# A two-layer hybrid backbone on one core: a different opening, loads moved to GpSimd's queue, and two spacings changed

## The chip, the cores and the metric

The kernel runs on one NeuronCore of a Trainium2 chip. The metric is the device time of one execution in microseconds. TensorE (PE) multiplies matrices, VectorE (DVE), ScalarE (ACT) and GpSimd (POOL) do elementwise work, and SyncE (SP), ScalarE and GpSimd issue DMAs, each into a queue of its own. An engine works through its instructions in the order of the program; an instruction that waits holds up all that stands behind it on that engine.

## The reference, cut to what matters

Two layers work on 256 context tokens and 256 latent tokens of width 1024. Each layer is a mixer of four branches and an MLP, both behind a modulated RMS norm. Context tokens go through the first layer whole; in the second only their scan states are needed.

```python
for l in range(DEPTH):                                  # DEPTH = 2
    mod   = c_act  @ w_mod[l] + b_mod[l]                # shift, scale, gate of both halves, latent tokens
    mod_c = cc_act @ w_mod[l] + b_mod[l]                # the same for context tokens
    hc = _modulate(xc, g_norm1[l], csh1, csc1)          # rms_norm(x, g) * (1 + scale) + shift
    zc = hc @ w_in[l]                                   # 1024 -> 5*256 branch inputs + 4*1024 gates
    ctx_states = _s5_states(zc[..., :256], *s5p, None)  # complex diagonal scan, both directions
    xc = xc + cga1 * _token_mixer(zc, ctx_states, p)    # (first layer only)
    xc = xc + cga2 * _sq_relu_mlp(_modulate(xc, g_norm2[l], csh2, csc2), mlp_w1[l], mlp_w2[l])
    h = _modulate(x, g_norm1[l], sh1, sc1)
    z = h @ w_in[l]
    lat_states = _s5_states(z[..., :256], *s5p, _s5_final(ctx_states))
    x = x + ga1 * _token_mixer(z, lat_states, p)        # S5, Fourier, pooling, convolution; gated, summed
    x = x + ga2 * _sq_relu_mlp(_modulate(x, g_norm2[l], sh2, sc2), mlp_w1[l], mlp_w2[l])
return _rms_norm(x, g_final)
```

The latent tokens get a 2-D position code added before the first layer.

## The kernel before

Activations lie transposed: 8 tiles of 128 channels by 512 tokens (context first, then latent), in `X`. Every large product takes three float32r products (high x high, high x low, low x high), so each weight tile (128 x 1024, 512 KB) is split after its load: ScalarE writes the high part, VectorE subtracts to get the low part. `Stream` does this for all weights in one fixed order with three raw buffers: `load` issues on SyncE's queue, `high` on ScalarE, and `low` on VectorE, which also frees the raw buffer for the next load. A low part is issued when its due time has come, or at the latest when `take` hands the weight to the products.

All instructions are put in order by the program itself. It keeps a clock for each engine ("t" TensorE, "d" VectorE, "a" ScalarE, "p" GpSimd), made of estimated costs. Between the products of a tile `pump` takes steps of background tasks, generators that say with `yield "w", x` that they want x us of TensorE's clock to pass, and that run when the clocks of their engines are less than a lead ahead of "t". So a step's place in every engine's queue follows from these estimates, and a wrong estimate shows up as an engine that stands still.

**The opening** (`run`, and the first part of `layer` for l = 0). x is loaded in four DMAs of two tiles, behind them weights and the 16 modulation pieces of 512 KB (`mod_load`, up to ten buffers). Position codes are added on VectorE, ScalarE squares, VectorE adds pairs, and each pair's sum goes to TensorE at once, which adds up all four pairs in one bank against a column of ones (`sums`). The norm's inverse root is a chain of small VectorE operations (`norm_steps`), and its broadcast goes over TensorE. `mod_part` multiplies one modulation piece; after each fourth, `mod_finish` turns the result into scale and shift of two of the eight tiles, which `h_tiles` needs to make the normed tiles. The first four column tiles of the input projection (two for S5, two for pooling) run k by k, as the tiles come: `group(k, *js)` does three products for each j. The order of groups, pieces, closings and tiles is written out by hand. `warm(n)` issues n products whose result isn't used.

**The first layer's mixer** goes through `order(0)`: gates (g), branch outputs (y) and projections (q), while background tasks make the branches. `S5.prep` (31 steps) makes the scan's discretised matrices, `tables_c` and `tables_b` (in rank order beside the others) its tables: four units u, for each of which a 64 KB piece of the C matrices is loaded (two buffers, SyncE's queue) and reloaded for u + 2 after unit u. The tables go out to DRAM. `S5L.run` starts when both are done. `states` loads the branch's input and four tables of 512 KB, into two buffers, on GpSimd's queue; the load for unit i + 2 is issued after the products of unit i. `mods_pe` computes the gate modulation of the first layer from eight pieces of 512 KB, one buffer, with a wait of 7.0 between a load and its products. `mods` does the rest of the modulation on VectorE until the MLP.

**The second layer's mixer** runs on the 256 latent tokens (context only for S5), so that a weight tile lasts half as long on TensorE, and its scan runs on VectorE beside the branches.

## Time and profile before

| | |
|---|---|
| time, median of 3 runs | 1208.14 us (1204.47 to 1208.62) |
| profiled execution: time, span, mean granted TensorE clock | 1212.6 us, 1210.8 us, 0.988 |
| TensorE busy | 1167.6 us, 96% |
| VectorE, ScalarE, GpSimd busy | 79%, 45%, 132.4 us |
| DMA | 211.50 MB, 175 GB/s on the mean |

A page of the profile gives the busy time of each engine (PEld is TensorE's load of the stationary operand, beside PE), the span in 40 slices and the costliest groups. The other views are asked for a stretch of time: a timeline of merged instructions, the list of waits, and tables of stretches with busy times and the granted clock. Nearly all instructions carry line 64, that of a helper that records them, so a group is told by the tiles that it reads and writes: "parts" are weight tiles and normed tiles, "mixer", "windows" and "scan" work areas, "whole" the area of x, raw weights and small things, "bank" PSUM. "in_..." and "scr_..." are tensors in DRAM.

### The profile page before, as it was taken

Reading aid. Unit: us, or ns where it says so; the run is one execution under the profiler, and the core shown is the slowest. Engines: PE = TensorE matmul, PEld = TensorE weight load, DVE = VectorE, ACT = ScalarE, POOL = GpSimd, SP = SyncE. Lnnn points to the kernel's source line nnn. Section 1 sums busy time; section 2 is a strip of 40 time slices with the busy share of each in tenths; the row PEclk is TensorE's granted clock in tenths of the full one; section 3 lists DMA queues with packets and bytes.
Section 4 is the critical chain, followed back from the end, with each engine's and each line's share of the span. In section 5 each row is a group of like instructions: output and inputs, shape, how many; then the busy total and the mean of one; then the engine's idle time right before and its main releaser. Section 6 shows DMA issues by size and latency. Waiting matters only on the chain. (4 is left out here: it accounts for less than half of the span.)

```text
span 1210.8 us, 20441 instructions
## 1 busy us (share of the span) xinstructions
PE 1167.6 (96%) x7900; PEld 1013.4 (84%) x7900; DVE 951.9 (79%) x1818; ACT 541.0 (45%) x1037; POOL 132.4 (11%) x134
## 2 busy tenths in 40 slices
PE   6899999999999999999999999999999999999997
PEld 5577676877877898888887778898989999999997
DVE  5587698997989768999988973557998788867764
ACT  4355543235333355332433442336644556645543
POOL 0010000000000100043324531030000002000000
PEclk9899999999999999999999999999999999999999
DMA  9363464337554603346777853435544546555551
GB/s 369 122 220 118 149 221 140 101 91 264 189 182 153 222 19 125 129 166 222 234 258 276 270 192 115 152 120 158 210 150 148 171 160 212 174 190 178 188 185 43
DMA packets 66370, 211.50 MB, mean 175 GB/s; under 512 B 7840, under 2 KB 13472, under 8 KB 66272
## 3 DMA queue, kind: packets, MB, share of 16 engines
q1 hardware_dynamic: 55456, 183.84, 44.7%
q10 hardware_dynamic: 7552, 14.56, 3.3%
q0 software_dynamic: 3264, 11.80, 2.9%
q8 instruction: 62, 1.02, 0.4%
q14 instruction: 36, 0.29, 0.1%
HBM read 199.19 MB, written 10.98 MB: 174 GB/s over the span
## 5 line engine op out<-in xcount | busy, mean ns | idle before, releaser
L64 PE MATMUL bank<-parts 128*128 128x512 f32 (+2 forms) x4008 | 728.0, 339 | 14.6 <-DVE parts L64 9.9
L64 PEld LDWEIGHTS bank<-parts 128*128 128x128 f32 x4008 | 613.1, 191 | 102.6 <-DVE parts L64 15.6
L64 ACT ACTIVATE parts<-whole 128x1024 fp32r<-128x1024 f32 (+1 forms) x288 | 273.6, 959 | 139.1 <-PE bank L64 63.5
L64 DVE TENSOR_TENSOR parts<-whole,parts 128x1024 fp32r<-128x1024 f32 (+1 forms) x240 | 292.2, 1225 | 16.0 <-ACT parts L64 15.3
L64 PE MATMUL bank<-hidden,parts 128*128 128x256 f32 (+1 forms) x1440 | 251.4, 335 | 0.0
L64 PEld LDWEIGHTS bank<-hidden,parts 128*128 128x128 f32 x1440 | 217.5, 188 | 29.7 <-issue 0.3
L64 DVE SCALAR_TENSOR_TENSOR whole<-whole 128x1024 f32<-128x1024 f32 (+3 forms) x174 | 158.5, 911 | 15.9 <-DMA whole<-in_w_modt_dram 12.8
L64 DVE SCALAR_TENSOR_TENSOR whole<-bank,whole 128x256 f32<-128x256 f32 (+1 forms) x121 | 54.8, 476 | 71.6 <-PE bank L64 71.6
L64 ACT ACTIVATE whole<-whole 128x256 f32<-128x256 f32 (+4 forms) x119 | 47.4, 423 | 96.7 <-DVE whole L64 96.3
L64 ACT ACTIVATE mixer<-bank 128x512 f32<-128x512 f32 (+1 forms) x84 | 40.6, 495 | 100.1 <-PE bank L64 92.9
L64 ACT ACTIVATE whole<-bank 128x512 f32<-128x512 f32 (+2 forms) x71 | 35.9, 527 | 106.2 <-PE bank L64 75.6
L64 DVE TENSOR_TENSOR whole<-whole 128x512 f32<-128x512 f32 (+7 forms) x154 | 62.7, 420 | 20.6 <-ACT whole L64 19.0
L64 POOL TENSOR_TENSOR whole<-whole 128x256 f32<-128x256 f32 (+2 forms) x42 | 30.1, 730 | 316.3 <-ACT whole L64 315.6
L64 DVE TENSOR_TENSOR hidden<-whole,hidden 128x512 fp32r<-128x512 f32 (+2 forms) x77 | 55.3, 722 | 9.4 <-ACT hidden L64 2.4
L64 ACT ACTIVATE hidden<-whole 128x512 fp32r<-128x512 f32 (+2 forms) x77 | 47.1, 615 | 6.5 <-PE bank L64 2.3
L64 DVE TENSOR_TENSOR scan<-scan 128x512 f32<-128x512 f32 (+3 forms) x51 | 28.4, 568 | 18.1 <-ACT scan L64 15.4
L64 DVE SCALAR_TENSOR_TENSOR scan<-scan,whole 128x512 f32<-128x512 f32 (+1 forms) x64 | 42.5, 733 | 0.0
L64 PE MATMUL bank<-merged,parts 128*128 128x256 f32 (+1 forms) x240 | 38.4, 317 | 1.3 <-DVE merged L64 1.3
L64 ACT ACTIVATE tables<-bank 128x512 f32<-128x512 f32 (+2 forms) x20 | 8.4, 420 | 67.5 <-PE bank L64 65.1
L64 POOL TENSOR_TENSOR whole<-tables 128x512 f32<-128x512 f32 x20 | 36.3, 1822 | 18.4 <-ACT tables L64 14.2
L64 PEld LDWEIGHTS bank<-merged,parts 128*128 128x128 f32 x240 | 33.8, 188 | 5.3 <-DVE merged L64 2.2
L64 DVE TENSOR_TENSOR mixer<-bank,mixer 128x512 f32<-128x512 f32 (+1 forms) x56 | 31.9, 575 | 7.5 <-PE bank L64 6.7
(109 smaller groups left out, 831.3 us busy)
## 6 DMA issues: line engine op xcount, KB each, us to landing
whole<-in_w_dram SPq DMA_DIRECT2D x128, 512.0 KB, 4.3
whole<-in_w_in_dram SPq DMA_DIRECT2D x84, 512.0 KB, 4.1
whole<-in_w_modt_dram SPq DMA_DIRECT2D x71, 512.0 KB, 4.3
whole<-in_w_br_dram SPq DMA_DIRECT2D x16, 512.0 KB, 3.9
whole<-in_w_out_dram SPq DMA_DIRECT2D x16, 512.0 KB, 4.1
mixer<-in_w_mod_dram SPq DMA_DIRECT2D x8, 512.0 KB, 8.2
whole<-in_w_modg_dram SPq DMA_DIRECT2D x8, 512.0 KB, 5.9
scan<-scr_b POOLq DMA_DIRECT2D x8, 512.0 KB, 6.3
```

Source lines behind the costliest of these rows:

```text
L64: return f(out, *a, **k)
```

## The change

- **Opening.** The position code of tiles 1, 3 and 5 is added on GpSimd, the sigmoid of the conditioning comes first, and the position tensor is loaded in two parts. The squares of all eight tiles are summed on VectorE into two accumulators, which TensorE then reduces in one go, behind two modulation pieces. The hand-written order of pieces, closings, tiles, groups and forced steps of S5's preparation is another; there are more warm products; the weights' loads come ahead of modulation pieces 4 to 7.
- **C matrices.** The first layer gets two more buffers, loads all four pieces at the start, and on GpSimd's queue.
- **Modulation pieces.** `mods_pe` loads on GpSimd's queue and waits 8.0 for a piece.
- **States.** In the first layer units 1 and 2 are followed by a wait of 5.0, not 1.0.
- **Low parts.** In the second layer's mixer a low part is due 0.5 after ScalarE's clock, where it was due 2.75 after TensorE's.
- A constant's load moves from the end of `mods` to the end of the first layer.

```diff
@@ -338,15 +338,17 @@
             CAs.append(K.MAT[:, 3072:3584])
+        else:
+            CCs += [A(128), A(128)]
         for BL in BLs:
...
         def load(u):
-            (nc.gpsimd if l else nc.sync).dma_start(CCs[u % 2], K.I["s5c"][l][u])
-
-        load(0)
-        load(1)
-        yield "w", 5.0 if l else 2.6
+            nc.gpsimd.dma_start(CCs[u % len(CCs)], K.I["s5c"][l][u])
+
+        for u in range(len(CCs)):
+            load(u)
+        yield "w", 5.0
@@ -372,11 +374,11 @@
             nc.scalar.dma_start(K.KD[l][64 * u:64 * u + 64], KK[0:64])
-            if u + 2 < 4:
-                load(u + 2)
+            if u + len(CCs) < 4:
+                load(u + len(CCs))
         def bufs(u, k):
-            CC = CCs[u % 2].rearrange("p (r k q c) -> p r k q c", r=2, k=2, c=16)
+            CC = CCs[u % len(CCs)].rearrange("p (r k q c) -> p r k q c", r=2, k=2, c=16)
             BL = BLs[u % nb].rearrange("p (k r q x) -> p k r q x", k=2, r=2, x=32)
@@ -499,7 +501,7 @@
                     nc.scalar.activation(o[:, :, ::-1] if k else o, pv[:, r, :, g], AF.Copy)
-            yield "w", 1.0
+            yield "w", 1.0 if l or i == 0 else 5.0
         if l == 0:
@@ -692,7 +694,7 @@
         self.ndma = self.nhigh = self.nlow = self.ntake = 0
-        self.used, self.due, self.lag = {}, [], 2.75
+        self.used, self.due, self.lag, self.early = {}, [], 2.75, False
@@ -717,7 +719,7 @@
                 self.nhigh += 1
-                self.due.append(self.K.nc.clock["t"] + self.lag)
+                self.due.append(self.K.nc.clock["a"] + 0.5 if self.early else self.K.nc.clock["t"] + self.lag)
                 return True
@@ -1105,7 +1107,6 @@
             yield "w", 3.02
-        nc.scalar.dma_start(self.MAT[:, 0:1792], self.I["const"][:, 264:2056])
         self.stream.free.append(self.MODRAW[0])
@@ -1117,8 +1118,8 @@
             for kp in range(4):
-                nc.sync.dma_start(raw, self.I["w_modg"][g][kp])
-                yield "w", 7.0
+                nc.gpsimd.dma_start(raw, self.I["w_modg"][g][kp])
+                yield "w", 8.0
                 for k in range(2):
@@ -1148,11 +1149,11 @@
...
-    def norm_steps(self, accs, n, width, d=None, pss=None):
+    def norm_steps(self, accs, n, width, d=None):
-        pss = pss or [self.aux() for _ in accs]
+        pss = [self.aux() for _ in accs]
@@ -1342,6 +1343,7 @@
         self.lead["d"] = 3.0 if l == 0 else 2.0
+        self.stream.early = l == 1
         s5 = S5L(self, l, self.pre[l])
@@ -1365,72 +1367,74 @@
-            prep = tab[0]
+            parts(2)
             weight(0)
-            norm = self.norm_steps((), 512, 1024, pss=[self.sums])
+            self.warm(1)
+            norm = self.norm_steps(((self.sq[1],), (self.sq[0],)), 512, 1024)
+            next(norm)
+            self.warm(2)
+            parts(1)
+            parts(1)
             y = [y for y in norm][-1]
-            parts(4)
+            self.warm(1)
+            self.mod_finish(0)
+            self.warm(2)
             d, r = self.tmp(), self.aux()
...
                 nc.tensor.matmul(r[:, sl], self.ones, d[:, sl], start=True, stop=True)
+            self.warm(4)
             h = self.h_tiles(l, 0, r, 0, 512)
             next(h)
-            self.mod_finish(0)
-            self.warm(2)
             next(h)
             group(0, 0)
+            self.stream.advance(1)
             self.mod_ahead = 16
             parts(1)
-            self.stream.advance(1)
             next(h)
             weight(1)
-            self.step(prep, 2)
+            parts(1)
             group(1, 0)
+            weight(2)
             parts(2)
             group(0, 1)
-            group(1, 1)
-            parts(1)
-            self.step(prep, 2)
             self.mod_finish(2)
             next(h)
-            self.stream.advance(1)
-            group(2, 0, 1)
             next(h)
-            parts(1)
-            weight(2)
-            self.step(prep, 2)
-            group(3, 0, 1)
-            parts(1)
+            group(1, 1)
             group(0, 2)
             group(1, 2)
+            self.step(tab[0], 3)
+            group(2, 0, 1, 2)
             parts(1)
-            self.stream.advance(1)
-            group(2, 2)
             weight(3)
-            self.step(prep, 2)
+            group(3, 0)
+            parts(1)
+            group(3, 1)
+            parts(1)
+            parts(1)
             group(3, 2)
-            parts(1)
-            group(0, 3)
+            self.step(tab[0], 4)
             self.mod_finish(4)
             next(h)
+            next(h)
+            group(0, 3)
             group(1, 3)
             group(2, 3)
-            next(h)
-            self.step(prep, 1)
             group(3, 3)
-            parts(1)
-            group(4, 0, 1, 2, 3)
+            self.step(tab[0], 3)
+            group(4, 0, 1)
             parts(2)
-            group(5, 0, 1)
-            parts(1)
-            self.step(prep, 2)
+            group(4, 2)
+            parts(2)
+            group(4, 3)
+            self.step(tab[0], 3)
             self.mod_finish(6)
-            group(5, 2, 3)
             next(h)
             next(h)
-            self.step(prep, 2)
+            self.step(tab[0], 3)
+            group(5, 0, 1, 2, 3)
             group(6, 0, 1, 2, 3)
@@ -1547,6 +1551,7 @@
         self.mod_need(l, 24)
+        self.stream.early = False
         self.lend_y(l + 1)
@@ -1645,6 +1650,7 @@
             nc.scalar.dma_start(self.SMW, self.I["smw"][1])
+            nc.scalar.dma_start(self.MAT[:, 0:1792], self.I["const"][:, 264:2056])
             self.turning = self.turn(l, 5, [("w2", l, 3, m) for m in range(4, 8)], *self.HID[1], 1, 0, (1, 0))
@@ -1742,13 +1748,14 @@
         mk = self.SCRA.mark()
-        pos = self.SCRA(272)
-        nc.scalar.dma_start(pos, I["pos"])
+        prow, pcol = self.SCRA(16), self.SCRA(256)
+        nc.scalar.dma_start(cc, I["cc"])
+        nc.scalar.dma_start(prow, I["pos"][:, 0:16])
+        nc.scalar.dma_start(pcol, I["pos"][:, 16:272])
         nc.scalar.dma_start(self.CONST[:, 0:264], I["const"][:, 0:264])
-        nc.scalar.dma_start(cc, I["cc"])
         nc.scalar.dma_start(self.PV[0][:, 0:142], I["pv"][0])
         self.pre = [S5(self, 0), None]
-        half = [self.A5.sub(3552), self.A5.sub(2656)]
+        half = [self.A5.sub(3136), self.A5.sub(3072)]
         self.tab0 = []
@@ -1757,44 +1764,38 @@
         self.tab0.append(self.start(make0(), "d", 0.0))
-        prep = self.tab0[0]
-        self.step(prep, 1)
+        self.step(self.tab0[0], 1)
         for k in range(0, 8, 2):
             nc.sync.dma_start(self.X[:, k:k + 2, :], I["x"][:, k:k + 2, :])
-        for ahead in (4, 8, 10):
-            self.stream.load()
-            self.mod_ahead = ahead
-            self.mod_load()
-            if ahead == 8:
-                self.step(prep, 1)
+        self.stream.load()
+        self.mod_load()
+        while self.stream.load():
+            pass
+        self.step(self.tab0[0], 1)
+        self.mod_ahead = 8
+        self.mod_load()
         nc.vector.memset(self.CACT, 0.0)
-        self.step(prep, 2)
+        self.step(self.tab0[0], 4)
+        self.warm(7)
         t = self.tmp()
-        pr = pos[:, 0:16].rearrange("p (k r) -> p k r", k=4)
-        pc = pos[:, 16:272].rearrange("p (k r) -> p k r", k=4)
-        self.warm(3)
-        self.sums = self.aux()
-        sq = [self.ACC if k == 0 else self.SIGR[k % 4] if k < 5 else self.TMP[k % 4] for k in range(8)]
-
-        def sums(k):
-            nc.vector.tensor_tensor(sq[k], sq[k], sq[k + 1], op=ADD)
-            for i in range(4):
-                nc.tensor.matmul(self.sums[:, i:i + 1], sq[k][:, 128 * i:128 * i + 128], self.ones[:, 0:1],
-                                 start=k == 0 and i == 0, stop=k == 6 and i == 3)
-
+        nc.scalar.activation(t[:, 0:16], cc, AF.Sigmoid)
+        nc.vector.tensor_tensor(self.CACT[:, :, 0:2], t[:, 0:16].rearrange("p (k c) -> p k c", c=2),
+                                cc.rearrange("p (k c) -> p k c", c=2), op=MUL)
+        pr = prow.rearrange("p (k r) -> p k r", k=4)
+        pc = pcol.rearrange("p (k r) -> p k r", k=4)
+        sq = []
         for k in range(8):
...
             pe = bc(pr[:, k, :, None], [128, 4, 64]) if k < 4 else bc(pc[:, k - 4, None, :], [128, 4, 64])
-            nc.vector.tensor_tensor(x, x, pe, op=ADD)
+            (nc.gpsimd if k in (1, 3, 5) else nc.vector).tensor_tensor(x, x, pe, op=ADD)
+            sq.append(self.ACC if k == 0 else self.SIGR[k % 4] if k < 5 else self.TMP[k % 4])
             nc.scalar.activation(sq[k], self.X[:, k, :], AF.Square)
-            if k == 1:
-                nc.scalar.activation(t[:, 0:16], cc, AF.Sigmoid)
-            if k % 2 and k > 1:
-                sums(k - 3)
-            if k == 3:
-                nc.vector.tensor_tensor(self.CACT[:, :, 0:2], t[:, 0:16].rearrange("p (k c) -> p k c", c=2),
-                                        cc.rearrange("p (k c) -> p k c", c=2), op=MUL)
-        sums(6)
+            if k in (3, 4):
+                nc.vector.tensor_tensor(sq[k - 3], sq[k - 3], sq[k - 1], op=ADD)
+        V = nc.vector.tensor_tensor
+        for i, j in ((1, 5), (0, 4), (1, 6), (0, 7)):
+            V(sq[i], sq[i], sq[j], op=ADD)
+        self.sq = sq[0:2]
         self.SCRA.reset(mk)
```

## Rows read from the trace of the kernel before

**Rows 1.** The page, busy time of each engine.
```profile
PE 1167.6 (96%) x7900; PEld 1013.4 (84%) x7900; DVE 951.9 (79%) x1818; ACT 541.0 (45%) x1037; POOL 132.4 (11%) x134
```

**Rows 2.** Waits of TensorE: waited for, us in total, times, longest.
```profile
PE bank L64 <- DMA whole<-in_w_modg_dram: 2.2, 2, 1.5
```

**Rows 3.** Stretches: length, busy PE, PEld, DVE, ACT, POOL; clock, DMA, GB/s.
```profile
6.80:12.60 5.80, 4.79 (x15) 3.62 (x15) 3.81 (x10) 5.75 (x9) 0.00 (x0) 1.00 1.03 416
24.69:66.10 41.41, 36.62 (x297) 24.76 (x298) 25.60 (x92) 17.79 (x31) 0.00 (x0) 0.92 0.48 185
34.90:41.70 6.80, 6.24 (x28) 3.92 (x27) 5.83 (x16) 3.47 (x6) 0.00 (x0) 0.50 0.48 172
137.30:140.70 3.40, 3.40 (x11) 2.63 (x10) 3.33 (x7) 3.32 (x13) 0.00 (x0) 0.50 0.20 77
901.90:905.30 3.40, 3.40 (x19) 3.40 (x18) 3.40 (x6) 0.00 (x0) 0.00 (x0) 0.50 0.90 301
```

**Rows 4.** Timeline of TensorE, first 25 us: start, us, instruction, idle before.
```profile
6.78 2.93 PE L64 MATMUL bank<-whole 128*128 128x256 f32 x6 [6.78 <-DMA whole<-in_x_dram]
...
16.03 2.85 PE L64 MATMUL bank<-whole 128*128 128x1 f32 x24
18.66 2.77 PE L64 MATMUL bank<-mixer,whole 128*32 128x128 f32 x48
...
24.69 0.50 PE L64 MATMUL bank<-parts 128*128 128x512 f32 x1 [1.09 <-ACT parts L64]
```

**Rows 5.** Timeline of TensorE, the rest of the opening.
```profile
32.53 0.39 PE L64 MATMUL bank<-whole 128*128 128x8 f32 x2 [0.40 <-ACT whole L64]
34.50 0.50 PE L64 MATMUL bank<-parts 128*128 128x512 f32 x1 [1.58 <-ACT parts L64]
...
42.41 1.66 PE L64 MATMUL bank<-parts 128*128 128x512 f32 x6
43.99 0.64 PE L64 MATMUL bank<-whole 128*32 128x128 f32 x16
...
72.42 24.36 PE L64 MATMUL bank<-parts 128*128 128x512 f32 x106 [0.84 <-DVE parts L64]
```

**Rows 6.** Timelines of SyncE, ScalarE and TensorE, 126 to 136 us.
```profile
126.70 4.58 SPq L345 DMA_DIRECT2D scan<-in_s5c_dram  x2
132.67 0.78 ACT L64 ACTIVATE scan<-scan 128x64 f32<-128x64 f32 x4 [5.64 <-DMA scan<-in_s5c_dram]
135.78 0.58 PE L64 MATMUL bank<-scan 128*32 128x112 f32 x8 [1.72 <-DVE scan L64]
```

**Rows 7.** The modulation pieces' landing; then DMA issues with KB and median landing.
```profile
DMA to landing us min/median/max: 3.3/5.9/11.1
...
scan<-scr_b POOLq DMA_DIRECT2D x8, 512.0 KB, 6.3
scan<-scr_z POOLq DMA_DIRECT2D x2, 512.0 KB, 9.0
```

**Rows 8.** Timelines of GpSimd and TensorE at the first layer's states.
```profile
188.38 0.70 POOL L64 DMA_DIRECT2D scan<-scr_b  x1 [25.11 <-PE bank L64]
194.95 1.68 PE L64 MATMUL bank<-scan 128*64 128x64 f32 x32 [2.62 <-DMA scan<-scr_b]
```

**Rows 9.** Timelines of VectorE and TensorE, end of the first layer's S5 branch.
```profile
329.57 1.28 DVE L64 TENSOR_TENSOR scan<-whole,scan 128x512 f32<-128x512 f32 x2
338.01 1.88 PE L64 MATMUL bank<-scan,whole 128*128 128x512 f32 x4
```

**Rows 10.** Timelines of ScalarE, VectorE and TensorE in the second layer's mixer.
```profile
896.27 1.05 ACT L64 ACTIVATE parts<-whole 128x1024 fp32r<-128x1024 f32 x1
900.25 1.22 DVE L64 TENSOR_TENSOR parts<-whole,parts 128x1024 fp32r<-128x1024 f32 x1
901.52 0.92 PE L64 MATMUL bank<-parts 128*128 128x256 f32 x4 [2.45 <-DVE parts L64]
...
987.24 0.98 PE L64 MATMUL bank<-parts 128*128 128x256 f32 x6 [1.33 <-DVE parts L64]
```

## Prediction, blind

> **What bounds the kernel now.** I read the page first: TensorE is busy 96% of the span [rows 1], so the only time to be had is what TensorE spends stopped or at the low clock. The second view is the list of what TensorE waited for (the line of it that the change names is [rows 2]); it gives the size of each kind of stop, and the timelines around them gave their places. The third is the table of stretches [rows 3]. After a stop of some 1.3 to 2.6 us the profile shows 3.4 us at a granted clock of 0.50 (1.2 instead of 2.4 GHz). There are five of these, of which the first and the last stand there; each costs 1.7 us more than its stop. One of 6.8 us lies in the opening and costs 3.4 us. So a stop of 2.5 us is worth about 4.2 us. The change touches three regions: the opening (to 66 us), the first layer's mixer (to 390 us) and the second layer's mixer (840 to 1000 us). I go through them in that order.
>
> The sum is made against the profiled execution: 1212.6 us, span 1210.8 us. The median of the timed runs, 1208.14 us, is 4.5 us below it, as much as 2.6 low-clock stretches of 1.7 us, so part of the clock losses in this trace is probably not in the median. That is taken off at the end.
>
> **Opening, before.** TensorE's first products run at the low rate, whatever the clock column says so early: six passes of 256 columns take 2.93 us, so 0.43 to 0.49 each, and a modulation piece (16 passes) takes 2.77 / 3 = 0.92 us against 0.57 later [rows 4, 5]. The sums of squares are 32 passes of one column at 0.21 us; the last eight start at 16.03 us, so they end near 17.7. The first product of the input projection starts at 24.69 [rows 4]; I call that T0. The end of the opening: the run of 106 products starts at 72.42 after a stop of 0.84, so the tile before it ended at 71.58; one 512-column product costs 24.36 / 106 = 0.230 us and that tile has 24, so the opening ended at 71.58 - 5.5 = 66.1 us [rows 5]. T0 to end: 41.4 us. The work in it: 96 products x 0.230 = 22.1; 12 pieces x 0.57 = 6.8; three closings of a group of pieces x 0.3 = 0.9; and about 12 restarts at 0.2 (six products take 43.99 - 42.41 = 1.58 from start to next start, against 6 x 0.230 = 1.38) = 2.4. Together 32.2. The other 9.2 us are stops (41.4 - 36.6 busy = 4.8), the low clock of 34.9 to 41.7 (3.4) and 1.0 of small change [rows 3].
>
> **Opening, after.** Only two accumulators are summed on TensorE: 2 x 4 x 2 = 16 passes, not 32, but all of them stand behind two modulation pieces and the last square. The 14 warm passes take 14 x 0.43 = 6.0 us and end at 12.8. Loads arrive at 416 GB/s [rows 3], 1.26 us for 512 KB: the first pair of x at 6.78, so the fourth at 10.6, the weight at 11.8, pieces 0 and 1 at 13.1 and 14.4 (estimates). Piece 1 ends near 15.5, one warm product follows, the sums start near 16.5. TensorE has little to do in the gaps before that, and the trace doesn't show that single-column passes raise the clock (before, 5 us of them did not speed up the pieces behind). At 0.21 us the sums end at 16.5 + 3.4 = 19.9; at the full rate, half that, 18.2. From the end of the sums to T0 it took 24.69 - 17.7 = 7.0 us before, with four pieces in between; now warm products, two pieces and the close of the first group lie there, and on VectorE three more small operations of 0.16 to 0.2 us stand ahead of the four scalings. At the low clock that is 8.5 us: T0 = 28.4, 3.7 later than before. At the full clock, with the sums started at 15.9 and without the wait for pieces, it is 6.2: T0 = 23.8. I take 28.4, since the rows show the low rate in this stretch; the far end is 30.2 if the clock rises only behind the broadcast.
>
> What the new order gives back comes behind T0. Each close of a group of pieces now has products behind it that are already possible (9, 12 and 12 of them, 2.1 to 2.8 us), where before the stop of 1.58 us stood bare [rows 5]. The chain to be hidden (close, two small VectorE operations, two ScalarE activations) took 34.50 - 32.53 = 1.97 us [rows 5], so I leave 1.2 us of stops in all, and no low-clock stretch. 32.2 + 1.2 = 33.4, and the end comes at 28.4 + 33.4 = 61.8, **4.3 us earlier** (8.9 with T0 = 23.8; 2.5 with 30.2; 0.9 later if 3.4 us of clock loss and another 1.8 of stops come back as well). GpSimd's three additions, the two separate position loads and the earlier sigmoid end before 16.5, so they cost nothing; additions of over 3 us each would show one for one.
>
> **C matrices.** The reload of C for the third unit is issued on SyncE's queue at 126.70, behind weight loads that wait for room. ScalarE stands still 5.64 us for it, VectorE behind ScalarE, and TensorE 1.72 us behind both [rows 6], then 1.7 us of low clock [rows 3]. With four buffers everything is loaded at the start and no reload is left: **-3.4 us**. What is late next is VectorE's own three operations of the unit, for which the planner leaves 0.5 us. Bounds: -3.4 to 0 (a first load that lands after its new 5.0 us would stop ScalarE in the same way).
>
> **States.** Unit 2 needs the table load that is issued only after unit 0's products, at 188.38, and TensorE stops 2.62 us for it [rows 8]; 1.7 us of low clock follow, one of the five. Two waits of 5.0 instead of 1.0 put unit 2 past 195. **-4.3 us**, -2.6 if the timed runs seldom had the clock loss. Price: the scan starts 8 us later. Its cover: this branch's gated activation is ready at 329.57 + 1.28 = 330.9 and TensorE's products on it start at 338.01, where the order forces them [rows 9]. That is 7 us of slack, and the tables end earlier (22 forced steps of the preparation in the opening, not 17), so I put nothing; without that cover it is 1 to 3 us.
>
> **Modulation pieces.** Eight loads of 512 KB move from SyncE's queue to GpSimd's, with 8.0 in place of 7.0 us to land. They cost two stops, 2.2 us [rows 2]. The trace has no such load on GpSimd's queue; the nearest rows are the 512 KB table loads there, median 6.3, and the scattered load of the scan's input, 9.0; on SyncE's they took 3.3 to 11.1, median 5.9 [rows 7]. On GpSimd they share the queue with the tables' and the scan's loads. Near 6.3, the stops go: -2.2. Near 9.0, each of eight stops 1.0 us: +8.0 less the 2.2 of before, +5.8. I take the table loads, which are contiguous like the pieces, and one bad meeting with the scan's load: **-1.0 us**.
> The rule that speaks against this edit is in the Trainium skill, DMA: Bandwidth & Descriptors, section SWDGE vs HWDGE vs iDMA: loads issued from GpSimd have their descriptors written by software, and VectorE can lock that out. By it alone the landing would be the longer one and this part +5.8 instead of -1.0. The medians of 6.3 and 5.9 [rows 7] agree with it in sign, but by 0.4 us only.
>
> **Second layer's mixer.** A weight's high part was ready at 896.27 + 1.05 = 897.3, its low part came behind four scan operations and a product at 900.25, and TensorE stopped 2.45 us; at 987.24 it stopped 1.33 us for another [rows 10]. The low part's due time was TensorE's planned clock + 2.75. A free ScalarE's clock stands about 1.05 ahead, so its clock + 0.5 is 1.55: 1.2 us earlier, which moves the low part ahead of at least one pair of scan operations. That takes 1.7 to 2.45 off the first stop and, once it is short, the 1.7 of clock with it; of the second about half. **-3.5 us**, bounds -5.5 and +1.0: VectorE works in order, so a low part issued before its high part is done holds up the scan and the gate products behind it.
>
> **Moved for nothing.** The constants' load moves from the end of the modulation work to the end of layer 0. It is one more issue on ScalarE's queue there, beside the load that stands there already, and its first reader is a branch of the next mixer. 0.
>
> **Sum.** -4.3 - 3.4 - 4.3 - 1.0 - 3.5 = -16.5 against the profiled execution. Of that, 8.5 are clock losses (3.4 in the opening, three stretches of 1.7); a third of these, 3 us, I take not to be in the median. 1208.1 - 13.5 = 1194.6, say 1195 us.
>
> **Rivals.**
> (1) The opening gives nothing: TensorE stays at 1.2 GHz through T0 and falls back once more. For it: the warm products end before the first piece lands, and two short stops follow. Then that part is +0.9 and the time 1195 + 5 = 1200.
> (2) The stops are dealt anew. The planner places all background steps by its own clocks, and these shift. If two stops like the one of 2.62 us [rows 8] arise elsewhere, each with its low clock, 8.6 us are lost again: 1204. For it: VectorE is busy 79% of the span [rows 1] and every stop found is one of order. Against it: the change takes away causes, not positions.
> (3) Slower: the pieces arrive late. Place: the eight pieces in the first mixer, in order on TensorE. It decides from a landing of 8.0 us. At 9.8 each stop is 1.8 and the clock falls behind each, 1.7: 8 x 3.5 = 28, less the other gains of 12: +16, and 1224 us. For it, the landing of 9.0 of the scan's load; against it, the table loads' 6.3 [rows 7]. The rule of the Trainium skill named above points to this rival; no row here shows it at work.
> (4) Better: the warm products bring the full clock before the sums and it stays. T0 = 23.8, 1190 us.
>
> **How the numbers follow.** Forecast (1190 to 1200) 0.55; (1) 0.14; (2) 0.17; (3) 0.06; (4) 0.08. A difference of 0.5%, 6 us, is about what a measurement of this kernel can tell from no change. Faster by more: the forecast, (1) and (4), 0.77. Within: (2), 0.17. Slower: (3), 0.06. The range takes in all but (3) and the ends of (2) and (4): 1185 to 1207.
>
> **What would show it.** In the profile after: no ScalarE stop of 5.6 us on the C load, no TensorE stop on the states' table load, at most one on the modulation pieces; T0 near 28 and the first long run behind the opening about 4 us before 72.4; fewer stops on weights' low parts between 840 and 1000 us. It would be wrong if TensorE stops for the pieces on most of the eight, if T0 to end stays near 41 us, or if stops of 2 us stand at new places.

## The result, and the profile after

The changed kernel takes **1192.66 us** (median of 4 runs, 1190.41 to 1194.26), the kernel before 1207.28 beside it (1204.47 to 1208.62): a ratio of 0.9881, 95% interval 0.9855 to 0.9906. The profiled execution took 1190.41 us, with a span of 1188.6 us. That pair of traces shows 22.2 us of difference where the medians show 14.6: the trace of before is 5.3 us above its median, that of after 2.3 below.

The page's busy line of TensorE and the list of what TensorE waited for (what, us in total, times, longest):

```profile
PE 1157.7 (97%) x7908; PEld 1006.7 (85%) x7908; DVE 950.6 (80%) x1818; ACT 540.3 (45%) x1036; POOL 142.7 (12%) x149
```
```profile
PE bank L64 <- DVE parts L64: 9.6, 10, 2.8
PE bank L64 <- DMA whole<-in_x_dram: 5.2, 1, 5.2
PE bank L64 <- DVE mixer L64: 2.6, 1, 2.6
...
PE bank L64 <- ACT merged L64: 1.4, 1, 1.4
PE bank L64 <- DVE merged L64: 1.1, 1, 1.1
```

The waits for the pieces [rows 2], the C reload behind VectorE's scan [rows 6] and the states' table load [rows 8] are gone. The 9.6 us of waits for weights' parts are not shorter (before: 9.9), and two waits on the merged products of the second layer are there, 1.4 and 1.1 us, where the kernel before had one of 0.87.

The opening: TensorE's timeline (start, length, instruction, in brackets the idle time ahead of it and what ended it), then stretches (length, busy PE, PEld, DVE, ACT, POOL; granted clock, DMA share, GB/s):

```profile
5.22 5.47 PE L64 MATMUL bank<-whole 128*128 128x256 f32 x14 [5.22 <-DMA whole<-in_x_dram]
13.27 1.08 PE L64 MATMUL bank<-whole 128*32 128x128 f32 x16 [2.57 <-DVE mixer L64]
...
16.41 0.99 PE L64 MATMUL bank<-whole,mixer 128*128 128x1 f32 x8
17.27 2.00 PE L64 MATMUL bank<-whole 128*128 128x1 f32 x12
...
24.83 0.49 PE L64 MATMUL bank<-parts 128*128 128x512 f32 x1 [0.17 <-ACT parts L64]
...
58.97 1.21 PE L64 MATMUL bank<-parts 128*128 128x512 f32 x4 [1.24 <-DVE parts L64]
```
```profile
13.09:16.50 3.41, 3.19 (x36) 2.17 (x36) 1.85 (x3) 0.10 (x1) 0.00 (x0) 0.50 1.03 420
24.83:57.00 32.17, 31.05 (x294) 22.92 (x295) 26.40 (x104) 17.16 (x31) 0.00 (x0) 1.00 0.59 231
126.00:200.00 74.00, 73.20 (x543) 56.92 (x538) 70.88 (x117) 32.03 (x93) 7.23 (x11) 1.00 0.52 172
968.00:976.00 8.00, 5.46 (x31) 5.03 (x30) 7.87 (x16) 6.01 (x11) 0.00 (x0) 0.79 0.37 124
```

To be seen here: the input landed at 5.22 (before 6.78 [rows 4], chance). The warm passes end at 10.7, TensorE stands 2.57 us, and the clock falls for 3.4 us. T0, the first product of the projection, comes at 24.83. From there the opening runs at 2.4 GHz almost without stops to about 57.0 (the stop ahead of 58.97 starts at 57.73 and lies ahead of the third product of the next tile; two products and the end of the last take some 0.7 back from there). In the first mixer (126 to 200) TensorE is busy 73.2 of 74 us; the two low-clock stretches that lay there are gone [rows 3]. Between 968 and 976 the clock falls again (0.79 on the mean).

By stage, the 22.2 us between the traces are: input 1.6; opening 6.7; from its end to the first layer's output projection 8.5; then 3.3 and 4.2 more by the end of layer 0, where two stops of TensorE for results of GpSimd are gone or short; and in the second layer 2.1 back, a loss. The two of GpSimd, in the list of waits of the kernel before:

```profile
PE bank L64 <- POOL tables L64: 2.6, 1, 2.6
...
PE bank L64 <- POOL whole L64: 1.5, 2, 1.3
```

After has no wait for the tables at all, and 0.5 us in all for the other.

### The profile page after: what moved, and what is told of

Its sections match the earlier page's. It is cut to its first block, busy times and chain, and to the rows that moved or that the text cites. A ratio compares the mean times of both kernels' runs of the same rounds, so it can differ in the third digit from the quotient of the medians.

```text
span 1188.6 us, 20465 instructions
## 1 busy us (share of the span) xinstructions
PE 1157.7 (97%) x7908; PEld 1006.7 (85%) x7908; DVE 950.6 (80%) x1818; ACT 540.3 (45%) x1036; POOL 142.7 (12%) x149
## 5 line engine op out<-in xcount | busy, mean ns | idle before, releaser
L64 PE MATMUL bank<-parts 128*128 128x512 f32 (+2 forms) x4008 | 719.2, 337 | 11.7 <-DVE parts L64 9.6
L64 DVE SCALAR_TENSOR_TENSOR whole<-whole 128x1024 f32<-128x1024 f32 (+4 forms) x172 | 154.3, 898 | 14.1 <-DMA whole<-in_w_modt_dram 10.9
L64 ACT ACTIVATE mixer<-bank 128x512 f32<-128x512 f32 (+1 forms) x84 | 40.6, 495 | 90.1 <-PE bank L64 76.3
L64 PE MATMUL bank<-whole 128*32 128x128 f32 (+4 forms) x276 | 30.4, 309 | 9.0 <-DMA whole<-in_x_dram 5.2
```

What stands on the lines that cost most here:

```text
L64: return f(out, *a, **k)
```

## The experiments

Since T0 scatters by the clock (below), the table also gives, from each trace, the time from the first product (it starts when the input lands) to T0, and from T0 to the end of the span. The last three columns split the latter: from T0 to the first product of the first layer's output projection (at 366.48 in after), from there to a stop of 0.81 us at the start of the second layer that every trace has (it ends at 807.47 in after), and from there to the end.

| kernel | median us | ratio to before, 95% | first product to T0 | T0 to end | T0 to output projection | to second layer | to end |
|---|---|---|---|---|---|---|---|
| before | 1207.3 | 1 | 17.9 | 1186.1 | 358.6 | 448.5 | 379.1 |
| after | 1192.7 | 0.9855 to 0.9906 | 19.6 | 1163.8 | 341.6 | 441.0 | 381.2 |
| e1: after again | 1191.1 | 0.9846 to 0.9907 | 18.5 | 1164.7 | 341.6 | 440.7 | 382.4 |
| e2: old opening | 1200.5 | 0.9921 to 0.9962 | 18.2 | 1176.7 | 348.4 | 447.1 | 381.2 |
| e3: low parts undone | 1192.5 | 0.9851 to 0.9903 | 20.0 | 1163.0 | 341.6 | 440.6 | 380.8 |
| e4: low parts, earlier of two clocks | 1192.5 | 0.9852 to 0.9905 | 18.7 | 1163.5 | 341.9 | 440.4 | 381.2 |
| e5: states undone | 1190.8 | 0.9837 to 0.9893 | 18.6 | 1165.1 | 341.8 | 441.3 | 381.9 |
| e6: C matrices undone | 1194.4 | 0.9863 to 0.9913 | 19.8 | 1165.0 | 342.0 | 441.4 | 381.6 |
| e7: pieces undone | 1195.9 | 0.9869 to 0.9926 | 24.3 | 1165.2 | 342.2 | 441.5 | 381.5 |
| e8: pieces on SyncE's queue, 8.0 | 1194.2 | 0.9850 to 0.9905 | 18.3 | 1163.3 | 341.6 | 441.2 | 380.5 |
| e9: opening alone | 1198.6 | 0.9900 to 0.9947 | 23.3 | 1168.0 | 348.0 | 440.4 | 379.6 |
| e10: mended | 1184.2 | 0.9775 to 0.9829 | 18.6 | 1158.7 | 340.1 | 441.1 | 377.4 |
| e11: before + C matrices | 1205.2 | 0.9941 to 0.9990 | 17.4 | 1184.7 | 355.1 | 448.4 | 381.2 |
| e12: before + states | 1206.1 | 0.9949 to 1.0000 | 18.3 | 1179.5 | 351.4 | 446.7 | 381.3 |

**e1, the change again**, and **e2, the opening as before** (the old blocks of the opening and its projection, all else as in the change).

> The changed kernel again, as the anchor for what is compared with it on this chip. All theories: 1192 to 1194 us beside 1207 to 1208 of the kernel before, ratio 0.988.

> The change with the opening of the kernel before; everything else stays. Theory A (each part is worth the stops it removes, read in its own place): the traces have the end of the opening 8.3 us earlier after the change, 1.6 of which lie before the first pair of x has landed and are chance; so 6.7 us come back and the time is 1199 to 1200 us. Theory B (the parts shift the planner's clocks, and the gain is that the later stops were dealt anew): undoing the opening deals all later stops anew, so the time can lie anywhere between 1192 and 1208, and the stops between 100 and 1000 us are at other places than in the changed kernel.

e1 gives the same time, and one difference that explains much of the scatter. Its opening:

```profile
13.11 0.64 PE L64 MATMUL bank<-whole 128*32 128x128 f32 x16 [2.91 <-DMA whole<-in_w_mod_dram]
...
23.71 0.50 PE L64 MATMUL bank<-parts 128*128 128x512 f32 x1 [0.18 <-ACT parts L64]
```

The stop is as long (2.91 us, 2.57 in after), but the piece behind it runs in 0.64 us, not 1.08: the clock, which rose at 8.7, stayed. e2's median is 9.3 us above e1's, near theory A's number. But its trace, 12.4 us longer than that of after, has only half of this where theory A puts it: 6.2 up to the layer's output projection (it starts at 372.70 against 366.48; 0.9 of that is the input's later landing). Another 6.1 lie between there and the second layer, where the stops for GpSimd's results near 410 (2.2 us, with its low clock), 614 and 661 (1.0 each) are back. So the opening decides these too: that stage takes 440.4 to 441.5 us in all ten traces with the new opening and 446.7 to 448.5 in the four with the old one.

**e3 and e4, the low parts.** e3 takes the new due time away, e4 takes the earlier of the two clocks:

```diff
-        self.stream.early = l == 1
+        self.stream.early = False
```
```diff
-   self.due.append(self.K.nc.clock["a"] + 0.5 if self.early else self.K.nc.clock["t"] + self.lag)
+   due = self.K.nc.clock["t"] + self.lag
+   self.due.append(min(due, self.K.nc.clock["a"] + 0.5) if self.early else due)
```

> The change with the low parts of the second layer's mixer due by TensorE's clock again (2.75). Theory A, as predicted: the part is worth 3.5 us, so 1196 us. Rival C (read from the trace after): where ScalarE is busy its clock is far ahead and the low part becomes due later, not earlier; the stop at the mixer's start was 1.51 us before and is 2.77 after, and the stops of that mixer add up to 8.2 us after against 6.0 at the same places before, so the part is worth nothing or less: 1190 to 1193 us, and the first stop of that mixer is 1.5 us again.

> The change with a low part due by the earlier of the two clocks (ScalarE's + 0.5, TensorE's + 2.75). Theory A: ScalarE's is the earlier one nearly always, so nothing changes, 1192 to 1193 us. Rival C: the low parts behind a busy ScalarE come 1 us earlier or more, the first stop of the second mixer falls from 2.8 to 1.5 us, and the second mixer's others at most stay: 1190 to 1191.5 us.

Neither moves the time (rival C's forecast for e3; for e4 it forecast 1 to 2.5 us less than was measured). The stops only change places. First after, then e3, then e4:

```profile
816.50 1.70 PE L64 MATMUL bank<-parts 128*128 128x256 f32 x12 [2.77 <-DVE parts L64]
...
878.72 1.45 PE L64 MATMUL bank<-parts 128*128 128x256 f32 x10 [1.26 <-DVE parts L64]
...
967.34 1.23 DVE L64 TENSOR_TENSOR parts<-whole,parts 128x1024 fp32r<-128x1024 f32 x1 [0.79 <-ACT parts L64]
...
969.40 0.42 ACT L64 ACTIVATE merged<-mixer 128x256 fp32r<-128x256 f32 x1 [2.09 <-DVE mixer L64]
...
971.39 4.85 PE L64 MATMUL bank<-merged,parts 128*128 128x256 f32 x25 [1.14 <-DVE merged L64]
```
```profile
879.26 4.13 PE L64 MATMUL bank<-parts 128*128 128x256 f32 x23 [2.42 <-DVE parts L64]
```
```profile
840.11 2.23 PE L64 MATMUL bank<-parts 128*128 128x256 f32 x14 [2.84 <-DVE parts L64]
```

The stop of 2.45 us [rows 10] shrinks to 1.26 with the change and is 2.42 without it: the edit does what it says there. It is given back twice. At the mixer's start ScalarE's clock is already far ahead (it has two long activations, three copies and three high parts queued), so its clock + 0.5 is later than TensorE's + 2.75, and the stop grows from 1.53 (e3) to 2.77. e4 has 1.54 there too, which shows this cause, but then stops 2.84 at the next weight. At the end the low part goes out too early: VectorE stands 0.79 us for its high part, the gate products wait behind it, ScalarE waits 2.09 us for those, and TensorE 1.39 and 1.14 (0.87 in all before), with 3.4 us of low clock.

Another stop, near 840, is not in the kernel before and does not come by this edit: it is 2.16 to 3.31 us with the old due time (e3, e9, e11, e12) and from under 0.3 to 2.84 with the new one (1.59 in after). In the kernel before one weight load, issued at 840.21, landed in 4.1 us; the same load took 7.1 to 7.7 us in after, e3 and e12, and VectorE then stood 4.0 to 6.1 us for ScalarE, not 1.3. Why it lands later is open; the moved load of the constants, which the prediction put at nothing, is in all of these kernels and was not undone by itself. So the second layer is longer than before with the old due time as well (380.8 in e3, 381.2 in e11, 381.3 in e12; 379.6 in e9, against 379.1).

**e5 to e8, the three parts of the first mixer undone one at a time** (the notes behind # are added here).

```diff
-            yield "w", 1.0 if l or i == 0 else 5.0      # e5
+            yield "w", 1.0
-            CCs += [A(128), A(128)]                     # e6: two buffers, SyncE's queue, 2.6
-            nc.gpsimd.dma_start(CCs[u % len(CCs)], K.I["s5c"][l][u])
+            (nc.gpsimd if l else nc.sync).dma_start(CCs[u % 2], K.I["s5c"][l][u])
-                nc.gpsimd.dma_start(raw, self.I["w_modg"][g][kp])   # e7; e8 keeps the 8.0
-                yield "w", 8.0
+                nc.sync.dma_start(raw, self.I["w_modg"][g][kp])
+                yield "w", 7.0
```

> The change with the states of the first layer spaced by 1.0 again. Theory A (each part is worth the stops of its own place): TensorE stops 2.6 us at unit 2 on the scr_b load again and 3.4 us at a clock of 0.5 follow in most executions: +2.6 to +4.3, 1194.5 to 1196 us. Theory B (what is gained is that later stops are dealt anew): the stop at unit 2 comes back, but the time differs from that of the change by another amount, because stops behind 200 us come or go; where TensorE's clock of the planner is the same behind the states, they can't, and then only A is left.

> The change with two buffers for the C matrices, loaded and reloaded on SyncE's queue. Theory A: the reload for the third unit stands behind weight loads, ScalarE stands still 5 to 6 us, TensorE 1.7 us, and the low clock follows in most executions: +1.7 to +3.4, 1193.5 to 1195.5 us. A rival: with the modulation pieces off SyncE's queue that queue is free sooner, the reload lands in time, no ScalarE stop over 2 us on it, and the time stays at 1191 to 1193 us.

> The change with the eight modulation pieces on SyncE's queue and a wait of 7.0. Theory A: two stops of TensorE on the pieces again, 1.4 to 2.2 us together, 1193 to 1194.5 us. A rival (the two stops came from the weights' and C loads that stood on the same queue): with the C loads gone from it the pieces land sooner, no stop is over 0.5 us and the time stays at 1191 to 1193 us.

> The change with the modulation pieces on SyncE's queue but with the wait of 8.0; beside the run before it, it tells the queue from the wait. If the queue is what counts (a piece stands behind a weight load that waits for room), the stops are those of the run before, within 0.5 us each. If the wait is, each stop is 1.0 us shorter and the time is that of the change, 1191 to 1193 us.

In time none of the four is clear of the change: ratios of 0.9865 to 0.9897, each with some 0.003 to either side, beside 0.9881 and 0.9876. The traces tell more. From T0 to the output projection, the stage of these parts, the four take 341.6 to 342.2 us, after and e1 both 341.6: undone alone, no part costs more than 0.6 us there, so the states don't lose their 4.3 nor the C matrices their 3.4. In e5 no wait for the table load appears, which neither theory had. In e6, whose median lies in theory A's range, the trace is nearly the rival's: ScalarE waits for the C load again, but only 2.03 us, and TensorE has no stop above 0.42 us between 100 and 190:

```profile
125.62 0.55 ACT L64 ACTIVATE scan<-scan 128x64 f32<-128x64 f32 x2 [2.03 <-DMA scan<-in_s5c_dram]
```

In e7 and e8 TensorE does not stop for any of the eight pieces. e7's higher median is not seen in that stage: in its profiled run the clock fell behind the warm passes and stayed low for 13.65 us, so that T0 came at 29.77. Whether its other runs lost their time in the same place is not shown.

```profile
13.88 1.08 PE L64 MATMUL bank<-whole 128*32 128x128 f32 x16 [3.27 <-DMA whole<-in_w_mod_dram]
...
29.77 0.50 PE L64 MATMUL bank<-parts 128*128 128x512 f32 x1 [0.17 <-ACT parts L64]
```
```profile
12.62:26.27 13.65, 12.33 (x92) 9.74 (x93) 5.72 (x22) 1.55 (x3) 0.00 (x0) 0.50 1.03 418
```

The pieces' time from issue to landing (minimum, median, maximum), on GpSimd's queue in after, then on SyncE's in e8:

```profile
DMA to landing us min/median/max: 3.6/4.3/5.5
```
```profile
DMA to landing us min/median/max: 3.3/5.6/7.7
```

**e9, all four undone together (the opening alone)**, and **e11 and e12, one part alone on the kernel before.** e9 has the edits of e3, e5, e6 and e7; e11 is e2 with those of e3, e5 and e7; e12 is e2 with those of e3, e6 and e7.

> The kernel before with the new opening alone (and the later load of the constants): C matrices in two buffers on SyncE's queue, pieces on SyncE's queue with 7.0, states spaced 1.0, low parts by TensorE's clock. Undone one at a time, each of these four cost nothing. Theory A, they are worth what the prediction gave them and only cover for each other (any one of them shifts the plan enough to keep the stops away): undone together they cost 9 to 12 us, since the stops of 1.7 on the C reload, 2.6 on the states' table load and 2.2 on the pieces come back with two or three stretches of 3.4 us at 1.2 GHz; 1200 to 1203 us. Theory B, the new opening alone moves the plan so that these stops don't arise: no stop above 1 us between 100 and 390 us, 1191 to 1195 us. In between, one of the three comes back, 1195 to 1198 us; the row that TensorE waits for says which.

> The kernel before with the C matrices alone in four buffers on GpSimd's queue (and the later load of the constants): everything else as before, the old opening too. Theory A, the term of the prediction holds where the plan is the old one: ScalarE's stop of 5.6 us and TensorE's of 1.7 us near 134 go, with the 3.4 us at 1.2 GHz behind them; -3.4, 1203 to 1205 us. Theory B, the reload only stood in a row with a modulation piece that waits on the same queue: TensorE stops for the piece instead, or the stop on the states' table load stays or grows; 1207 to 1209 us. If C alone shifts the plan so that the states' stop goes too: 1198 to 1201 us.

> The kernel before with the wider spacing of the states alone (and the later load of the constants), old opening. Theory A, the term of the prediction holds in the old plan: no TensorE stop of 2.6 us on the states' table load near 192 and no 3.4 us at 1.2 GHz behind it, -2.6 to -4.3; 1202 to 1205 us. Theory B, that stop stood only on where the plan put the load, and the wider spacing moves both: it stays, or another of 2 us comes; 1206 to 1209 us. From the new opening alone the stop was gone with the old spacing, which speaks for B about the cause, but doesn't say what the spacing does in the old plan.

e9 costs some 5 to 6 us against the change (1198.6 against 1192.7, the ratios 0.42% apart). In the traces it loses 6.4 us from T0 to the output projection, and gets some 2 back behind it, most of it in the second layer. SyncE's, ScalarE's, TensorE's and VectorE's timelines and two stretches show it:

```profile
122.09 2.07 SPq L708 DMA_DIRECT2D whole<-in_w_in_dram  x2
124.29 0.43 SPq L345 DMA_DIRECT2D scan<-in_s5c_dram  x1
125.21 0.33 SPq L1119 DMA_DIRECT2D whole<-in_w_modg_dram  x1
...
129.87 0.54 ACT L64 ACTIVATE scan<-scan 128x64 f32<-128x64 f32 x2 [2.69 <-DMA scan<-in_s5c_dram]
...
131.13 0.64 PE L64 MATMUL bank<-whole 128*32 128x128 f32 x16 [1.48 <-DMA whole<-in_w_modg_dram]
...
144.30 0.96 PE L64 MATMUL bank<-scan 128*32 128x112 f32 x8 [2.94 <-DVE whole L64]
```
```profile
131.87 0.69 DVE L64 TENSOR_TENSOR scan<-scan 128x512 f32<-128x512 f32 x1 [3.64 <-PE bank L64]
...
141.82 2.35 DVE L64 TENSOR_TENSOR parts<-whole,parts 128x1024 fp32r<-128x1024 f32 x2
...
144.09 0.16 DVE L64 TENSOR_TENSOR whole<-bank,whole 128x8 f32<-128x8 f32 x1
```
```profile
126.00:200.00 74.00, 69.58 (x501) 54.17 (x500) 62.55 (x106) 29.75 (x96) 5.31 (x7) 0.95 0.54 178
141.30:150.30 9.00, 6.06 (x42) 5.20 (x41) 4.72 (x8) 2.79 (x10) 0.00 (x0) 0.62 0.70 208
```

A piece and the C reload stand side by side in SyncE's queue, behind two weight loads, and land at 131.08 and 129.85. In the kernel before it is the same pair (issued at 126.24 and 126.70). That they meet is not what makes them slow: in this place a piece takes 5.7 to 6.2 us from issue to landing without the C load beside it (e7, e8, e11) and 5.9 to 6.3 with it (before, e9, e12). TensorE stops 1.48 us for the piece. The larger loss is the second stop, 2.94 us, with 6.8 us of low clock: TensorE waits for a small operation of VectorE that stands behind two low parts (144.09), and VectorE itself had stood still 3.64 us until 131.87, while both loads were out. With either load alone on the queue TensorE waits for the same operation, 0.42 us (e6) and 0.99 (e7), and for neither load. That VectorE's lateness comes from the two loads fits this, but the steps between are not shown. Neither theory of e9 held whole: a stop on the pieces is back, the stop behind VectorE's scan [rows 6] isn't, and the stop on the table load doesn't come although the spacing is the old one.

In the old plan the terms hold in the sum, but not as one stop for each edit. e11, then e12:

```profile
189.88 1.64 PE L64 MATMUL bank<-scan 128*64 128x64 f32 x32 [3.63 <-DMA scan<-scr_b]
```
```profile
134.16 0.96 PE L64 MATMUL bank<-scan 128*32 128x112 f32 x8 [1.72 <-DVE scan L64]
```

With the C matrices alone the stop at 134 shrinks to 0.5, but the stop on the table load grows from 2.62 [rows 8] to 3.63, and of the two stops on the pieces [rows 2] 0.40 us are left; in time, 0.9965 x 1209.15 - 1209.15 = -4.2 us (interval -1.2 to -7.1). With the states alone the stop on the table load is gone, and the longer one on the pieces with it; the one at 134 stays as it was [rows 6]; -3.0 (0.0 to -6.2, so hardly clear of no change, and at the edge of theory B's range, as e11 is at the edge of theory A's). The traces say it more sharply. From the first product behind the opening (at 65.5) to the output projection the kernel before takes 317.7 us, e11 3.4 less, e12 5.8 less, and e2, with the three edits together, 9.2 less. The pieces alone on the kernel before were not tried.

**e10, the change mended by these readings.**

```diff
-        self.stream.early = l == 1
+        self.stream.early = False
...
             group(4, 2)
+            self.stream.advance(1)
             parts(2)
...
         tconv = self.start(br.conv(), "d", 4.0)
+        self.stream.early = l == 1
...
                 if b == 0:
+                    self.stream.early = False
                     self.lead["d"] = 2.0
...
-        self.warm(7)
+        self.warm(12)
```

> The change with three edits by what the traces show. (a) 24 warm passes, not 14: the load of the first piece lands 2.5 us behind the last warm pass, the clock falls and stays low for 3.4 us. If the stop is the cause, the clock stays at 2.4 GHz from the first rise on and T0 comes 1 to 2 us earlier than in the change, 22.5 to 24; if it is not, T0 stays near 24.8 or comes later. (b) One weight's high and low part is taken earlier in the opening: the stop of 1.24 us near 57.7 goes. (c) ScalarE's clock gives the due time of the low parts only between the convolution's start and the last branch's product: the stops of 2.77 near 814 and of 1.4 and 1.1 near 969 (with the low clock behind them) give way to 1.5 near 814 and at most 1.3 near 964, and the one near 877 stays at or below 1.3. All three right: 1191 - 1.5 - 1.2 - 1.2 - 2.5 = 1184 to 1186 us. If the plan deals the stops out anew, as it did for every part undone so far: 1189 to 1193 us.

**1184.19 us** (1183.80 to 1185.05), 0.9802 of before: faster than both, and in the range expected of all three edits. TensorE's timeline and waits:

```profile
5.03 7.00 PE L64 MATMUL bank<-whole 128*128 128x256 f32 x24 [5.03 <-DMA whole<-in_x_dram]
13.03 0.65 PE L64 MATMUL bank<-whole 128*32 128x128 f32 x16 [1.00 <-DVE mixer L64]
...
23.62 0.50 PE L64 MATMUL bank<-parts 128*128 128x512 f32 x1 [0.18 <-ACT parts L64]
...
838.41 2.77 PE L64 MATMUL bank<-parts 128*128 128x256 f32 x21 [2.29 <-DVE parts L64]
...
875.59 2.66 PE L64 MATMUL bank<-parts 128*128 128x256 f32 x20 [1.29 <-DVE parts L64]
...
959.46 4.33 PE L64 MATMUL bank<-parts 128*128 128x256 f32 x34 [1.33 <-DVE parts L64]
...
966.58 3.62 PE L64 MATMUL bank<-merged,parts 128*128 128x256 f32 x28 [0.88 <-DVE merged L64]
```
```profile
PE bank L64 <- DVE parts L64: 9.0, 9, 2.3
...
PE bank L64 <- DVE merged L64: 0.9, 1, 0.9
```

The clock rises at 8.2 and stays up until the tail (1179.0), as in no other trace but e5's. The stop of 1.24 near 58 is gone, those at 969 and 971 give way to 1.33 and 0.88, and the one at 879 stays at 1.29. From T0 on it takes 5.1 us less than the change. The wait for weights' parts is still 9.0 us; the longest of these stops is now the one near 838 (2.29 us; 1.59 in after, 2.16 in e3). The five runs lie within 1.3 us, where the change's ten in both series span 7.1; that 24 warm passes end the scatter of T0 fits this, but was not tried by itself.

## Why the prediction was right, point by point

The forecast of 1195 us was 2.3 above the median, and the reason is partly the one given. That it came so near is partly luck: two misses stand against each other, 7.5 us gained behind the opening that stand in no term, and 5.6 us in the second layer, where -3.5 was forecast and the traces show +2.1. By its own terms, against the traces:

- **Opening, T0: the case that it took did not come in this trace, and the case changes from run to run.** It gave 28.4 at the low clock and 23.8 at the full one, from the input at 6.78; that is 21.6 and 17.0 us from the first product. Traces with the new opening show the first product to T0 taking 18.3 to 18.7 us where the clock stayed (e1, e4, e5, e8, e10), 19.6 to 20.0 with 3.4 us of low clock (after, e3, e6), 23.3 and 24.3 with 10.2 and 13.7 us (e9, e7). So both of its sums are 1.3 us or more too short, and that T0 stands at 23.6 to 23.8 in the first five, as rival (4) has it, is luck: the input landed 1.3 to 1.8 us earlier. In after T0 came at 24.83, 3.6 us before the forecast. The step to blame is "I take 28.4": it took one clock for the whole stretch and for every run.
- **Opening, from T0 on: right.** Predicted 33.4 us; measured 57.0 - 24.83 = 32.2, with 1.1 us idle where 1.2 was left for stops, and no low clock. The end of the opening before was read 0.8 too late: its stop stood ahead of the third product of a tile, not of the first, so the opening ended near 65.3 and T0 to its end took 40.6, not 41.4. The gain of the stage, 6.7 from the input's landing on, lies between the 4.3 taken and the 8.9 of the far end.
- **Opening, behind its end: missed.** Two stops for GpSimd's results, 1.33 and 2.56 us with 1.7 of low clock each, are gone or under 0.8 us with the new opening and near their old places with the old one (e2, e11, e12): 7.5 us that stand in no term. The opening runs more of the first layer's preparation; that this is what lets GpSimd's later work start sooner is not shown. e9 gives the opening alone, with the later load of the constants, 0.0077 x 1208.79 = -9.3 us.
- **First mixer: right as a sum, wrong as a sum of parts.** -3.4 - 4.3 - 1.0 = -8.7 was predicted and the traces show -8.5. On the old opening the traces give C alone -3.4, the states alone -5.8 and all three -9.2 (e11, e12, e2). On the new one each can be undone for 0.6 us or less, and all together cost 6.4 up to the output projection (e9); pairs were not tried. The step that failed is the premise that each stop has a cause of its own. The pieces' stop of 1.45 us goes with C alone, with the states alone and with the opening alone; the stop on the states' load doesn't come behind the new opening even with the old spacing (e9), and grows with C alone (e11). Which step of the plan brings each stop is not shown.
- **Pieces: the landing was sooner than taken, the worth of the part is not shown.** I took a landing of 6.3 us on GpSimd's queue; it was 4.3, with 5.5 the longest, so rival (3), which needs over 8.0, never came near. But undone alone the part costs nothing that the runs can tell (e7, e8), the stops it was to remove go with other parts, and it was not tried by itself on the kernel before. SyncE's pieces took 5.6 (e8). Over all traces, a piece that SyncE issued with two weight loads in flight took 6.2 us on the median, with one 4.5, with none 3.1 to 4.3; GpSimd's took 4.4, nearly always with one or none. The rule of the Trainium skill, DMA: Bandwidth & Descriptors, section SWDGE vs HWDGE vs iDMA, gives SyncE's loads the faster setup. With no weight load in flight the traces agree in sign (a median of 3.4 us against 4.4, but of four pieces only); what the loads ahead add is more.
- **Low parts: wrong.** Predicted -3.5 with bounds -5.5 to +1.0. The part is worth nothing in time (e3). The second layer as a whole lost 2.1 us between the traces, but with the old due time it loses as much (1.7 to 2.3 us in e3, e11 and e12), by the stop near 840. The failed step is "a free ScalarE's clock stands about 1.05 ahead": it isn't free at the mixer's start, so the low part came later there. The upper bound named the other half, VectorE held by a low part that is ahead of its high part, but gave it 1.0 where stops and clock at 969 cost 3.4.
- **Clock.** 3 us were taken off for clock losses in the trace that the median doesn't have. The trace of before stands 5.3 us above the median of its runs here, so the step was right, if small; the granted clock, 0.988 in that trace and 0.990 or 0.991 in the medians of three of four later series, accounts for 2.4 to 3.6 us of it. The price of 1.7 us behind a stop is an average: in the kernel before, stops of 1.45, 1.51 and 1.33 us (at 171, 840 and 987) have no low clock behind them.
- **Rival (2), stops dealt anew**, fits much of this, with the sign mostly the other way: 7.5 us less behind the opening, and a stop of 1.59 us more near 840. The other losses in the second layer, some 4.6 us (2.77 - 1.51 at 814, and 1.39 + 1.14 - 0.87 at 969 with 1.7 of clock), are not dealt anew but the due time's own, since e3 doesn't have them.

## What to carry to other kernels

A stop that a planner's order produces has no price of its own: undo each edit alone and do it alone before adding up, since one stop may go with any of several edits, and one edit may lengthen another's stop. A due time taken from an engine's planned clock moves with that engine's backlog, later where it is busy; use it where the engine is free, and don't let an in-order engine take a step ahead of its input. And where a kernel's times scatter, compare traces by stage and mend the stage that differs.

## What the runs showed of the hardware

The length of a stop didn't decide whether TensorE's clock fell behind it. With the new opening and 14 warm passes it stayed at 2.4 GHz over stops of 2.8 to 3.0 us in four traces, where it had risen at 8.7 or 8.8 (e1, e4, e5, e8), and fell behind stops of 2.5 to 3.3 us in five, where it had risen at 9.2 to 10.3 (after, e3, e6, e7, e9). It then stayed low for 3.4, 10.2 or 13.7 us while TensorE was busy nearly all the time (12.33 of 13.65 us in e7). What sets the moment of the rise, the runs don't say. It is the same later on: behind a stop of 2.77 to 2.79 us near 815 the clock stayed up in four traces (after, e5, e7, e8), and was low for 3.4 us in e2 and e6 and for 6.8 us in e1.

Loads of 512 KB issued by GpSimd landed sooner than the same loads on SyncE's queue (median 4.3 us in after against 5.6 in e8; medians of 3.7 to 4.6 in eight traces against 5.2 to 6.0 in six). What goes with it is how many weight loads are in flight at the issue: two for 21 of SyncE's 48 pieces, which took 5.6 to 7.9 us, and for one of GpSimd's 64. With one in flight the two queues hardly differ (medians of 4.5 and 4.4 us).
